# Routing and NSA stages of a hybrid decoder layer: zeros written by ScalarE, the second gate's modulation moved, products issued in pairs, other issue orders

## The chip, the cores and the metric

One core of a Trainium2 chip runs the whole layer as one program. The metric is device microseconds (us) of one execution. The engines are TensorE (PE in the profile, with its weight loads as PEld), VectorE (DVE), ScalarE (ACT), GpSimd (POOL), SyncE (SP, which only issues DMAs here). Each engine runs its own queue in the order in which the program put the instructions; an instruction that waits holds up all that stand behind it on its engine.

## The reference

512 tokens of width 1024 pass through one layer in fp32. Cut to its outline:

```python
mod = silu(c) @ ada_w + ada_b
sh1, sc1, gt1, sh2, sc2, gt2 = split(mod, 6)
h = ln(x) * (1 + sc1) + sh1
z = h @ w_in                          # columns of three mixers
o_a = mla_attention(...)              # 4 heads
o_b = banded_window_attention(...)    # 4 heads, window 128, sinks
o_c = nsa_attention(...)              # 8 heads, 2 KV groups: g0*compressed + g1*selected + g2*window
x = layernorm(ALPHA * x + (1 + gt1) * (concat[o_a, o_b, o_c] @ w_out))
h = ln(x) * (1 + sc2) + sh2
x = layernorm(ALPHA * x + (1 + gt2) * moe(h))   # 16 experts in 4 groups, one group, two experts of it
```

The selected branch of NSA takes for each query the 8 best of 16 key blocks; here it is computed densely, over all causal keys with a mask. The router's choice decides which expert sees which token.

## The kernel before

The tokens stand in four blocks of 128 (n = 0 to 3). The stages follow each other: modulation and layer norm, projections with MLA and window attention, the NSA stage (function `nsa(n)`, queries of a block by `queries(n)`), the output projection with the second layer norm and the routing of each block (`outproj(n)`, which calls `route(n)`), and the experts (a loop over four expert groups q). A scheduler turns the program into one queue for each engine: it goes by program order, shifted by priorities (`pri`, whose numbers stand in `PRM`), by what is ready in its own model of time, and by free buffers. `tc.issue_after(ins)` puts what follows behind `ins` on the same engine. The order of the stages' pieces is the string `ORD`: q is a query block, n an NSA block, o an output block, s steps of the first modulation iterator, g steps of `gstep`; what stands behind Z comes after the buffers of the projections are freed.

In `nsa(n)` the 8 heads fall into two groups g. For each block: window scores (L849) and softmax; `nl`, the choice of blocks and the masks `msk` (L882); `np`, the window part of the output, with products of V and the transposed probabilities (function `pv`, L894); then for g = 0 and 1 in turn the selected part: scores (L921), softmax into the tile `Sg` (L490, L491, scaled in L133), for each key block kt four transposes (`stp`, L501), their copy from PSUM into a tile `pt` (L127), and `pv`. All products of a block add up in one PSUM bank (`onsa`), group 0 in partitions 0 to 63 and group 1 in 64 to 127: each `pv` uses 64 of the array's 128 columns. The products with `vz` are the compressed branch.

The second gate (gt2, needed at the end of the experts) is `m3`: two steps of `mod_half`, each with two groups of four matmuls (`gemv`, L323, `modps`) on four loaded tiles of ada_w (`ada`, L192) and two additions on VectorE (L548). The tiles come from the pool `zraw` (tag w, 5 buffers), which also holds the raw halves of W_out (`wo`, L966) for its split into `woh` and `wol`, the gate tile gt1, and later gt2 and four tiles `x1g`. The two steps are called by `step(16, gsteps)` behind the last output block. `s2 s1 s2 s2` in the last part of `ORD` call an iterator that has six steps, all of which have been taken by then.

`outproj(n)` multiplies the heads' outputs by W_out (`yps`, L1215: `oM` part in fp32, `oN` part split in `oh` and `ol`), normalizes on VectorE (L1217 to L1233), transposes (`x1p`), copies to `x1T` on ScalarE, computes the router's logits (`lps`, `lsum`) and writes the normalized rows to DRAM (`t2`, L1238 and L1240). `route(n)` is a chain of some fifty small VectorE instructions with three products on TensorE between them: `rkp` (ranks, L1097), `tabp` (L1129) and `tabq` (L1163, L1165). After block 3, `tokB` (L1131) lists the tokens of the experts' second and third slots. `warm` adds products whose result nobody reads.

The experts' loop gathers rows (`gather`, an indirect DMA of POOL, L1289) into the tiles `rows`, transposes them (`gTp`), and computes gate and up (`gu`, L1319: for each of 8 k, for each of 3 slots b, four matmuls side by side), then down (`dn`). Slot b = 0 holds tokens of the first two blocks and is known after block 1 (`tokA`); b = 1 and 2 need `tokB`. The rows of a gather that no token fills must be zero: POOL clears `rows` 1 and 2 (L1272) and the first two pairs of `x1g` (L1327, L1328).

## Time and profile before

| | us |
|---|---|
| median of 3 runs | 593.4 |
| the runs | 591.91, 593.4, 599.62 |
| the profiled execution | 596.7 |
| its span, first to last instruction | 594.8 |
| busy in the span: PE, DVE, ACT, POOL | 548.7, 368.2, 222.1, 97.4 |
| NSA stage and output projection with routing of the first blocks | 234 to 384.6 |
| last block's norm and routing, up to its first expert product of slot 1 | 384.6 to 423.3 |
| experts | 423.3 to 584 |

The execution that was profiled took 596.7 us; 1.9 us of it lie around the span. A busy PE counts the modelled ends of pipelined matmuls, so neighbouring matmuls overlap in the sums of single durations; the busy time of a stretch counts each moment once. A matmul in fp32 stands as two records.

### The profile page before, as it was taken

Reading aid. Unit: us, or ns where it says so; the run is one execution under the profiler, and the core shown is the slowest. Engines: PE = TensorE matmul, PEld = TensorE weight load, DVE = VectorE, ACT = ScalarE, POOL = GpSimd, SP = SyncE. Lnnn points to the kernel's source line nnn. Section 1 sums busy time; section 2 is a strip of 40 time slices with the busy share of each in tenths; the row PEclk is TensorE's granted clock in tenths of the full one; section 3 lists DMA queues with packets and bytes.
Section 4 is the critical chain, followed back from the end, with each engine's and each line's share of the span. In section 5 each row is a group of like instructions: output and inputs, shape, how many; then the busy total and the mean of one; then the engine's idle time right before and its main releaser. Section 6 shows DMA issues by size and latency. Waiting matters only on the chain.

```text
span 594.8 us, 10444 instructions
## 1 busy us (share of the span) xinstructions
PE 548.7 (92%) x3856; PEld 333.1 (56%) x3856; DVE 368.2 (62%) x1219; ACT 222.1 (37%) x556; POOL 97.4 (16%) x114
## 2 busy tenths in 40 slices
PE   2899999999899999999899999978899999999990
PEld 1559775687788998755455456653434234234240
DVE  7515656664678568877769568886138157167174
ACT  2514443561428336374634512121434062070130
POOL 0114200000010010003301112123502122011022
PEclk9969999999799999999999999978999999999996
DMA  8993246743930200098300685359699999999601
GB/s 301 373 328 108 83 142 225 260 153 102 323 91 19 72 37 1 2 220 226 124 2 0 222 278 200 119 209 306 164 370 351 366 365 348 374 356 354 248 1 47
DMA packets 77546, 117.05 MB, mean 197 GB/s; under 512 B 7937, under 2 KB 54440, under 8 KB 77492
## 3 DMA queue, kind: packets, MB, share of 16 engines
q1 hardware_dynamic: 72328, 102.60, 52.9%
q0 software_dynamic: 4960, 13.64, 6.3%
q8 instruction: 32, 0.52, 0.4%
q14 instruction: 22, 0.18, 0.1%
q10 hardware_dynamic: 204, 0.11, 0.1%
HBM read 112.12 MB, written 8.40 MB: 203 GB/s over the span
## 4 chain that ended last, share of the span: by engine, by line
PE 78%; DVE 11%; issue 3%; DMA 3%; ACT 2%; POOL 2%; ACTq 0%; POOLq 0%
PE gu L1319 13%; PE zps L407 13%; PE dn L1370 7%; PE onsa L894 6%; PE yps L1215 5%; PE zall L423 3%; PE modps L323 2%; PE modps L375 2%; PE gTp L997 2%; PE cmb L1410 2%; PE stp L501 2%; PE sps L921 2%; PE wps L849 1%; PE warm L356 1%; PE cmh L1418 1%
## 5 line engine op out<-in xcount | busy, mean ns | idle before, releaser
L1319 PE MATMUL gu<-gu,gT 128*32 128x512 f32 x768 | 85.3, 596 | 0.1
L1319 PEld LDWEIGHTS gu<-gu,gT 128*32 128x32 f32 x768 | 23.8, 110 | 52.5 <-issue 50.6
L1370 PE MATMUL dn<-dn,aT 128*32 128x512 f32 x384 | 45.3, 597 | 0.4 <-ACT aT L127 0.2
L1343 DVE TENSOR_TENSOR act<-act,gu 128x256 f32<-128x256 f32 x12 | 5.1, 421 | 59.8 <-ACT act L1342 59.8
L1002 ACT ACTIVATE gT<-gTp,modc,modc 128x128 f32<-128x128 f32 x96 | 35.7, 461 | 10.1 <-PE gTp L997 9.5
L1342 ACT ACTIVATE act<-gu 128x256 f32<-128x256 f32 x12 | 4.6, 387 | 72.1 <-PE gu L1319 72.1
L1215 PE MATMUL yps<-wol,oM 128*128 128x512 f32 x64 | 30.9, 595 | 0.0
L1375 DVE SCALAR_TENSOR_TENSOR y<-dn,tab,gt 128x512 f32<-128x512 f32 x24 | 18.0, 748 | 10.2 <-PE dn L1370 10.2
L323 PE MATMUL modps<-ada,cond 128*32 128x512 f32 x128 | 18.3, 631 | 4.4 <-DVE gr L1079 4.1
L1370 PEld LDWEIGHTS dn<-dn,aT 128*32 128x32 f32 x384 | 10.4, 109 | 20.8 <-issue 18.5
L894 PE MATMUL onsa<-pt,vs 128*64 128x512 f32 x40 | 20.6, 614 | 0.0
L491 ACT ACTIVATE Sg<-Sg,nms 128x128 f32<-128x128 f32 (+3 forms) x32 | 17.8, 559 | 3.7 <-DVE nms L490 3.3
L491 ACT ACTIVATE W<-W,nmw 128x256 f32<-128x256 f32 (+1 forms) x32 | 15.3, 478 | 9.7 <-DVE nmw L490 9.3
L997 PEld LDWEIGHTS gTp<-cf,rows 128*128 128x128 f32 x96 | 10.4, 142 | 15.1 <-ACT gT L1002 9.2
L448 DVE TENSOR_TENSOR rp<-zps,trig 128x128 f32<-128x128 f32 (+1 forms) x28 | 9.7, 345 | 12.9 <-PE zps L407 12.5
L356 PE MATMUL warm<-cf 128*128 128x128 f32 x88 | 17.2, 326 | 0.1
L407 PE MATMUL zps<-B1s,hH 128*128 128x256 f32 x64 | 15.1, 329 | 2.2 <-DVE B1s L210 1.1
L356 PEld LDWEIGHTS warm<-cf 128*128 128x128 f32 x88 | 13.8, 222 | 5.5 <-issue 4.7
L1378 DVE TENSOR_TENSOR ys<-y,ys 128x512 fp32r<-128x512 f32 x22 | 15.2, 692 | 2.1 <-ACT ys L127 1.4
L997 PE MATMUL gTp<-cf,rows 128*128 128x128 f32 x96 | 14.8, 282 | 1.6 <-DMA rows<-xs_d,tokB 1.6
L127 ACT COPY pt<-stp 128x512 f32<-128x512 f32 x14 | 7.9, 586 | 22.2 <-PE stp L501 21.9
L1389 ACT ACTIVATE R<-R,rsf 128x1024 f32<-128x1024 f32 x3 | 3.7, 1241 | 31.4 <-DVE rsf L1388 31.4
(529 smaller groups left out, 1472.7 us busy)
## 6 DMA issues: line engine op xcount, KB each, us to landing
ada<-in_ada_w_dram SPq DMA_DIRECT2D x48, 512.0 KB, 5.9
gu<-in_moe_w_gate_dram SPq DMA_DIRECT2D x32, 512.0 KB, 9.7
gu<-in_moe_w_up_dram SPq DMA_DIRECT2D x32, 512.0 KB, 9.6
dn<-in_moe_w_down_dram SPq DMA_DIRECT2D x16, 1024.0 KB, 10.5
x<-in_x_dram SPq DMA_DIRECT2D x4, 512.0 KB, 4.9
phik<-in_nsa_phi_k_dram SPq DMA_DIRECT2D x4, 512.0 KB, 5.0
phiv<-in_nsa_phi_v_dram SPq DMA_DIRECT2D x4, 512.0 KB, 4.8
wo<-in_w_out_dram SPq DMA_DIRECT2D x8, 256.0 KB, 9.3
```

The source lines that it names most:

```text
L323: return lambda: PE.matmul(ps[32 * j:32 * j + 32], cond[:, k], t[:, 512 * (j % 2):512 * (j % 2) + 512], start=first, stop=last, skip_group ...
L356: PE.matmul(ps[:, :128], ident, ident, start=True, stop=True)
L407: PE.matmul(ps[:, :w], l[:, k, ts_], get(k, r), start=(k == 0 and i == 0), stop=(k == KD - 1 and i == 2))
L423: m = PE.matmul(outs[n], l[:, k, n * 128:(n + 1) * 128], get(k, r), start=(beg and n % 2 == 0), stop=(k == KD - 1 and i == 2), skip_group_ ...
L491: S.activation(S_h, S_h, AF.Exp, bias=nm, scale=-1.0, accum_out=den)
L894: PE.matmul(ops[64 * g:64 * g + 64, cols], lhsT, rhs, start=first[g], stop=False, skip_group_check=True)
L997: PE.transpose(ps[:, k * 128:(k + 1) * 128], src[:, (4 * a + k) * 128:(4 * a + k + 1) * 128], ident)
L1002: S.activation(dst[:, kk], pk, AF.Identity, bias=sh2(kk), scale=sc2(kk))
L1215: last = PE.matmul(ps, l, r[:, cs], start=(i == 0), stop=(i == len(order) - 1))
L1319: together([lambda e=e: PE.matmul(gu[b][32 * e:32 * e + 32], gT[b][:, k, 32 * e:32 * e + 32], w[:, e], start=(k == 0), stop=(k == KD - 1), ...
L1370: together([lambda b=b, e=e, f=f: PE.matmul(dn[b][32 * e:32 * e + 32], aT[b][:, f, 32 * e:32 * e + 32], wd[f][:, e], start=(f == 0), stop= ...
L1375: V.scalar_tensor_tensor(y, dn[b], tab[:, s:s + 1], gt2[:, cs], op0=OP.mult, op1=OP.mult)
```

## The change

ScalarE writes the zeros (as a product of a constant tile with 0.0) that POOL wrote. The second gate's two steps are taken as `g1` before and after the NSA block 2 in `ORD`; the first call of `gstep` flushes the first iterator and makes `m3`. The empty steps go. In `nsa(n)` the selected part computes the scores and the softmax of both groups first and then, for each key block, transposes both and issues the two products one behind the other (`pv2`); the window and compressed products are tied in pairs too. The `pt` tiles in the NSA stage become four, the mask tiles two. `t2` on ScalarE is issued behind the copies to `x1T`. The gate and up products of q = 0 with k >= 3 are issued behind the last `tabq` product.

```diff
-    "ORD": "q0 q1 n0 n1 q2 q3 s1 n2 Z n3 o0 s2 s1 s2 o1 o2 s2 o3 L", "SWb": 2, "WF": 2, "aTe": "S", "c10": -600,
+    "ORD": "q0 q1 n0 n1 q2 q3 s1 g1 n2 g1 Z n3 o0 o1 o2 o3 L", "SWb": 2, "WF": 2, "aTe": "S", "c10": -600,
...
-    "gst1": 80, "gst2": 40, ... "mskb": 3, ... "ptbs": 2, "ptbw": 2,
+    "gst1": -40, ... "mskb": 2, ... "ptbs": 4, "ptbw": 4,
...
                 def pv(g, lhsT, rhs, cols):
-                    PE.matmul(ops[64 * g:64 * g + 64, cols], lhsT, rhs, start=first[g], stop=False, skip_group_check=True)
+                    m = PE.matmul(ops[64 * g:64 * g + 64, cols], lhsT, rhs, start=first[g], stop=False, skip_group_check=True)
                     first[g] = False
+                    return m
+
+                def pv2(v, pts, cols):
+
+                    m = pv(1, v[:, 64:128], pts[1], cols)
+                    with tc.issue_after(m.ins), tc.high_priority():
+                        pv(0, v[:, 0:64], pts[0], cols)
...
                     pts = [tposed(qp, SW[g][:, :, b * 128:(b + 1) * 128], "wtp") for g in range(2)]
-                    for g in range(2):
-                        pv(g, vw[:, w0 + b, 64 * g:64 * g + 64], pts[g], slice(0, 512))
+                    pv2(vw[:, w0 + b], pts, slice(0, 512))
...
                 for r in range(4):
-                    for g in range(2):
-                        pv(g, vz[:, 4 * g + r], cpt, qs(r))
-
+                    m = pv(0, vz[:, r], cpt, qs(r))
+                    with tc.issue_after(m.ins), tc.high_priority():
+                        pv(1, vz[:, 4 + r], cpt, qs(r))
+
+            Sgs = []
             for g in range(2):
...
-                    for kt in range(n + 1):
-                        pt = tposed(qp, Sg[:, :, kt * 128:(kt + 1) * 128], "stp")
-                        pv(g, vs[:, kt, 64 * g:64 * g + 64], pt, slice(0, 512))
+            with pri(f"nv{n}"):
+                for kt in range(n + 1):
+                    pts = [tposed(qp, Sgs[g][:, :, kt * 128:(kt + 1) * 128], "stp") for g in range(2)]
+                    pv2(vs[:, kt], pts, slice(0, 512))
...
+        gsteps = []
+
+        def gstep(n):
+
+            if not gsteps:
+                step(16)
+                gsteps.extend((mod_bias(10, 2), 0))
+                gsteps[1] = mod_half(gsteps[0], 1)
+            step(n, gsteps[1])
...
-        m3 = mod_bias(10, 2)
-        gsteps = mod_half(m3, 1)
...
-            warm(f"wT{n}", PE.matmul(tq[:, 2 * NSLOT:2 * NSLOT + 8], ohg, rg, start=False, stop=True, skip_group_check=True))
+            tabq.append(PE.matmul(tq[:, 2 * NSLOT:2 * NSLOT + 8], ohg, rg, start=False, stop=True, skip_group_check=True))
+            warm(f"wT{n}", tabq[-1])
...
-                    cp(pick("x1T", "SS", hf), x1T[:, 4 * hf:4 * hf + 4], heads(ps, 4))
+                    x1c = S.copy(x1T[:, 4 * hf:4 * hf + 4], heads(ps, 4))
...
-            S.activation(t2, x1, AF.Identity, bias=nm, scale=rs2)
+            with tc.issue_after(x1c.ins):
+                S.activation(t2, x1, AF.Identity, bias=nm, scale=rs2)
...
+        def zero(dst):
+
+            S.mul(dst, cf[:, :dst.shape[-1]], 0.0)
+
         for r in rows_[1:]:
-            G.memset(r, 0.0)
+            zero(r)
         cnt_w = [0]
-        step(16, gsteps)
-        gate_out(1, m3)
+        gstep(16)
+        gate_out(1, gsteps[0])
...
-                for b in range(CAPB):
-                    together([lambda e=e: PE.matmul(gu[b][32 * e:32 * e + 32], gT[b][:, k, 32 * e:32 * e + 32], w[:, e],
-                                                    start=(k == 0), stop=(k == KD - 1), skip_group_check=True)
-                              for e in range(4)])
+
+                with tc.issue_after(tabq[-1].ins) if q == 0 and k >= 3 else nullcontext():
+                    for b in range(CAPB):
+                        together([lambda e=e: PE.matmul(
+                            gu[b][32 * e:32 * e + 32], gT[b][:, k, 32 * e:32 * e + 32], w[:, e],
+                            start=(k == 0), stop=(k == KD - 1), skip_group_check=True) for e in range(4)])
...
                 if q < 2:
-                    G.memset(x1g, 0.0)
-                    G.memset(x2g, 0.0)
+                    zero(x1g)
+                    zero(x2g)
```

## Rows read from the trace of the kernel before

**Rows 1.** The page: busy time of PE and DVE in the span, and the chain that ended last by engine.
```profile
PE 548.7 (92%) x3856; PEld 333.1 (56%) x3856; DVE 368.2 (62%) x1219; ACT 222.1 (37%) x556; POOL 97.4 (16%) x114
...
PE 78%; DVE 11%; issue 3%; DMA 3%; ACT 2%; POOL 2%; ACTq 0%; POOLq 0%
```

**Rows 2.** Busy time by stretch: bounds, length, then busy us (instructions) of PE, PEld, DVE, ACT, POOL, the granted clock of TensorE, DMA share and GB/s.
```profile
234.00:384.60 150.60, 147.01 (x762) 88.42 (x760) 113.80 (x470) 64.56 (x166) 29.04 (x28) 1.00 0.45 133
384.60:402.50 17.90, 13.83 (x107) 8.68 (x107) 15.02 (x71) 5.41 (x12) 4.17 (x6) 0.81 0.58 214
402.50:408.70 6.20, 3.53 (x32) 1.46 (x24) 5.93 (x19) 1.29 (x2) 4.18 (x6) 1.00 0.99 326
408.70:416.20 7.50, 7.44 (x46) 3.58 (x46) 3.58 (x32) 0.00 (x0) 0.00 (x0) 0.77 1.06 331
416.20:423.30 7.10, 5.39 (x49) 4.23 (x45) 2.33 (x11) 0.90 (x3) 3.62 (x6) 1.00 0.54 126
```

**Rows 3.** Groups of TensorE instructions by line in the stretch 243 to 347: busy us, mean ns of one, idle before.
```profile
L894 PE MATMUL onsa<-pt,vs 128*64 128x512 f32 x40 | 20.6, 614 | 0.0
...
L501 PE MATMUL stp<-cf,Sg 128*128 128x128 f32 x80 | 12.7, 283 | 1.6 <-DVE Sg L133 1.6
...
L894 PE MATMUL onsa<-pt,vw 128*64 128x512 f32 x28 | 11.3, 618 | 0.0
...
L894 PE MATMUL onsa<-cpt,vz 128*64 128x128 f32 x64 | 6.3, 284 | 0.0
...
L1215 PE MATMUL yps<-woh,oh 128*128 128x512 f32 x14 | 6.2, 440 | 0.0
```

**Rows 4.** Timeline of TensorE: products of both groups side by side, one product alone, all eight products of a compressed branch, eight transposes.
```profile
282.33 1.08 PE L894 MATMUL onsa<-pt,vw 128*64 128x512 f32 x4
...
294.24 1.07 PE L894 MATMUL onsa<-pt,vs 128*64 128x512 f32 x2
...
286.73 1.09 PE L894 MATMUL onsa<-cpt,vz 128*64 128x128 f32 x16
...
299.07 1.09 PE L501 MATMUL stp<-cf,Sg 128*128 128x128 f32 x8
```

**Rows 5.** Timeline of ScalarE: a copy of transposed probabilities from PSUM.
```profile
341.60 0.59 ACT L127 COPY pt<-stp 128x512 f32<-128x512 f32 x1 [1.80 <-PE stp L501]
```

**Rows 6.** Timeline of TensorE: the first two entries of the second gate's products, and the last block's logits.
```profile
384.63 1.92 PE L323 MATMUL modps<-ada,cond 128*32 128x512 f32 x16
...
390.63 1.94 PE L323 MATMUL modps<-ada,cond 128*32 128x512 f32 x8 [4.07 <-DVE gr L1079]
...
399.58 0.64 PE L1244 MATMUL lps<-x1T,rwc 128*32 128x128 f32 x16
```

**Rows 7.** VectorE instructions on the tile `mod` in the stretch 384.6 to 402.5 (columns as in rows 2, without ACT and POOL).
```profile
384.60:402.50 17.90, 0.00 (x0) 0.00 (x0) 3.14 (x5) 0.81 0.58 214
```

**Rows 8.** Timeline of ScalarE around the last block's copies.
```profile
394.02 1.24 ACT L1238 ACTIVATE t<-yt,ynm,yrs 128x1024 f32<-128x1024 f32 x1 [10.19 <-DVE key L1099]
...
395.17 1.05 ACT L127 COPY x1T<-x1p 128x512 f32<-128x512 f32 x2
```

**Rows 9.** Timeline of VectorE: `aff` in block 2's routing and in block 3's, the last inputs of block 3's products, and its token list.
```profile
384.17 0.17 DVE L1142 TENSOR_SCALAR aff<-th 128x16 f32<-128x16 f32 x1
...
402.63 4.08 DVE L1142 TENSOR_SCALAR aff<-th 128x16 f32<-128x16 f32 x1
...
411.80 0.23 DVE L1157 TENSOR_SCALAR r<-oht,gr 128x24 f32<-128x24 f32 x1
...
416.87 0.17 DVE L1131 TENSOR_TENSOR tokB<-tab,tabp 128x12 int32<-128x12 f32 x1 [4.45 <-PE tabp L1129]
```

**Rows 10.** Timeline of POOL: the first two and the last of the six memsets.
```profile
402.10 1.86 POOL L1272 MEMSET rows<- 128x1024 f32 x2
...
406.14 0.54 POOL L1328 MEMSET x1g<- 128x512 f32 x1
```

**Rows 11.** Timeline of TensorE from block 3's `rkp` products to its `tabp`, without some entries between.
```profile
405.65 0.38 PE L1096 MATMUL rkp<-asg,ones 128*128 128x20 f32 x2
...
408.76 0.40 PE L1097 MATMUL rkp<-asg,cf 128*128 128x20 f32 x2 [2.73 <-DVE asg L1088]
...
410.18 2.50 PE L356 MATMUL warm<-cf 128*128 128x128 f32 x10
...
414.36 1.92 PE L1319 MATMUL gu<-gu,gT 128*32 128x512 f32 x16
...
416.21 0.61 PE L1129 MATMUL tabp<-rh,ohp 128*128 128x12 f32 x4
```

**Rows 12.** The chain of waits at the gather, and all gathers into `rows`: from issue to landing.
```profile
417.79 4.25 DMA rows<-xs_d,tokB
...
DMA to landing us min/median/max: 4.2/6.2/7.1
```

**Rows 13.** Timeline of SP's queue: the later seven loads of W_out's raw halves, and the second gate's tiles.
```profile
257.82 6.33 SPq L966 DMA_DIRECT2D wo<-in_w_out_dram  x7
...
278.13 14.59 SPq L192 DMA_DIRECT2D ada<-in_ada_w_dram  x4
...
385.33 2.19 SPq L192 DMA_DIRECT2D ada<-in_ada_w_dram  x4
```

More of the change, by code (lines that the diff above doesn't have):

```diff
@@ L910, in nsa @@
                 for r in range(4):
-                    for g in range(2):
-                        pv(g, vz[:, 4 * g + r], cpt, qs(r))
+                    m = pv(0, vz[:, r], cpt, qs(r))
+                    with tc.issue_after(m.ins), tc.high_priority():
+                        pv(1, vz[:, 4 + r], cpt, qs(r))
+            Sgs = []
             for g in range(2):
                 with pri(f"ns{n}"):
-                    Sg = qp.tile([128, 4, 512], F32, name="Sg", bufs=pr("Sgb", 2))
+                    Sg = qp.tile([128, 4, 512], F32, name="Sg", bufs=2)
+                    Sgs.append(Sg)
                     nm, dn = tiny("nms"), tiny("dns")
@@ L938, in run @@
                     f[t[0]][0](int(t[1]))
-        outproj = gstep = None
+        gsteps = []
[5 more added lines that the diff above has]
+            step(n, gsteps[1])
+        outproj = None
         ORD = pr("ORD", "q0 n0 q1 n1 s1 q2 q3 Z n2 n3 L o0 o1 o2 g1 o3 g1")
@@ L1057, in build @@
         base = rp.tile([128, 20], F32, name="base")
+        tabq = []
         def route(n, lps, rs):
```

4 lines of the change are left out of this document (1 added, 3 removed), and 6 rows, old and new, of the table PRM.

## The prediction, made before the changed kernel was run

> **What bounds the kernel now.** I read the page first: TensorE is busy for 92% of the span and holds 78% of the chain that ended last [rows 1]. Such a mean hides stages with other limits, so the next view is the busy time by stretch. From 234 to 384.6 us (NSA, output projection, routing of the first blocks) TensorE is busy for 147.0 of 150.6 us, VectorE for 113.8 [rows 2]. The reader is to see that there an engine's work counts, not a chain's latency: a microsecond of TensorE saved is a microsecond at most, while VectorE leaves room. In the 38.7 us from 384.6 to 423.3 it is the other way round. That is block 3's norm and routing, and nothing but its end (the token list, the gather, the transposes) lets the experts go on. There the waits count: VectorE is busy for 15.0 of 17.9 us and then for 5.9 of 6.2, then it idles while TensorE is busy, then both wait for a DMA [rows 2]. The experts behind 423.3 are left as they are, so what is won before moves them forward as a whole.
>
> **The products in pairs.** One product of 64 columns takes 1.07 us alone, and two of different groups take 1.08 us together [rows 4]. The selected part's 20 products are all issued alone or behind one of the same group: 20.6 us busy (40 records). As ten pairs they take 10 x 1.08 = 10.8, so 9.8 less. The 14 window products take 11.3 us; seven pairs are 7.6, so 3.7 less. The compressed products take 6.3 us; four branches at the best one's 1.09 are 4.4, so 1.9 less [rows 3, 4]. Together 15.4; some of these intervals overlap (the three groups add up to 38.2 us, and the moments counted once are a little fewer), so I take 14.7.
>
> **The gate's modulation, moved.** In the NSA stretch TensorE gets four groups of four matmuls more; two take 1.92 us [rows 6], so 3.8. VectorE gets 3.1 us there [rows 7]. Eight loads of 512 KB go with it on SP's queue; four were issued in that stretch already, at 278, and held four of the five `zraw` buffers until 384.6, four at 385.3 [rows 13]. The DMA share of the stretch is 0.45 [rows 2], so transfer time is covered; what it costs if the buffers run out is the rival below. Net for TensorE: 14.7 - 3.8 = 10.9 us.
>
> How much of that is time? Now both softmaxes of a block must be finished before the first selected product, so the first group's products no longer cover the second group's softmax. Transposes wait 1.6 us for the scaled `Sg` once in the old order [rows 3]; I charge about 1 us for each of four blocks, 4 us. VectorE would hold 113.8 + 3.1 = 116.9 us in some 140, still below TensorE. So the stretch gives **7 us**. Bounds: nothing, if the new waits eat all, and 10.9, the whole of the work.
>
> **Block 3's norm.** The moved work leaves the stretch 384.6 to 402.5: 3.1 us on VectorE, which is busy there for 15.0 of 17.9, and on TensorE products behind a wait of 4.07 us, with the norm's transposes queued behind them [rows 2, 6]. The wait is put to a VectorE instruction; I read it as the four tiles issued at 385.3 [rows 13]. The first group after it took 1.94 us where two groups had taken 1.92; the granted clock is 0.81 in this stretch [rows 2, 6]. Here ScalarE also wrote `t2` (1.24 us) before the copies to `x1T`, and the logits came at 399.58 [rows 6, 8]; now the copies go first, and the write of `xs_d` starts some 1 us later, 20 us before it is read. Bounds: nothing, if the interleaved routing of block 2 sets the pace, and 6, the two waits behind `modps` with the 1.24. VectorE's is the nearest row: **3.5 us**.
>
> **The zeros.** `aff` took 0.17 us in block 2 and 4.08 in block 3, from 402.63 to 406.71, and POOL's six memsets run from 402.10 to 406.68 [rows 9, 10]. VectorE stood still for them, 3.9 us. With ScalarE writing they go. ScalarE has 1.29 us of work in 402.5 to 408.7 and none in the 7.5 us after it [rows 2]; six products of at most 1.24 us (the 1024 wide activation [rows 8]) are under 7.5 us and are covered, unless one is issued before the routing's own tanh, which then waits 1.2. TensorE has products queued before `rkp` until 406.0 [rows 11], so `rkp` moves from 408.76 to 406.0 at best: **3 us**, bounds 0 (if it meets the next wait at once) and 3.9. The Trainium skill ("SBUF — State Buffer", section SBUF: two separate sides) says that VectorE and GpSimd take the shared port pair as an exclusive lock for one whole instruction. By that alone the wait would be one memset, some 1 us, and the sum 2 us smaller, which lies inside the main case. The rows show VectorE passed over for all six.
>
> **The products held back.** `tabp`'s inputs are there at 412.0, and it starts at 416.21: 12 `warm` records and `gu` products of slot 0 with k = 3 to 6 stand before it [rows 9, 11]. With k >= 3 behind `tabq`, only the warm ones (2.5 us for ten) stand between `rkp` and `tabp`: **4.1 us**. The five `gu` groups held back (16 records 1.92, so about 5 us) then fall into the wait for the gather; if TensorE's clock is at its half level then, they take up to 10.
>
> **What they collide with.** The gather took 4.25 us, in a stretch with a DMA share of 0.54; in the 14 us before it the share is 0.99 to 1.06, with weights, gate and norm rows on SP's queue [rows 2, 12]. That traffic starts when block 3's buffers go free, so it does not move against the routing, but the gather comes some 7 us earlier relative to it and meets its last part. Gathers into `rows` have a median of 6.2 and a maximum of 7.1 us [rows 12]: I give back **2 us**, bounds 0 and 2.9.
>
> The other edits (empty steps, mask and `pt` buffers) move no work; four `pt` tiles let a pair wait for its two copies without holding up the next transposes.
>
> **Sum.** 7 + 3.5 + 3 + 4.1 - 2 = 15.6 us. Against the profiled execution's 596.7 us that is 581.1. That execution lies 3.3 us above the median of 593.4, and the runs spread from 591.9 to 599.6, so against the median it is **578 us**.
>
> **Rivals.**
> *Only the routing gains.* NSA's new waits eat the pairs: For it: the selected transposes do wait for `Sg`; against it: TensorE has output products to fill with, some 18 us of the split kind alone before 347 (three kinds of 14 records, 6.2 us for one [rows 3]). Then 8.6 us are left: 585.
> The Trainium skill ("TensorEngine Tiling (Array Packing)", section PSUM Bottleneck) says that side by side products speed up TensorE but not the copies out of PSUM, which may become the bound. As a mechanism here: a pair needs two copies of 0.59 us, 1.2 us on ScalarE alone, while its transposes and products take 2 x 1.09 + 1.08 = 3.3 us on TensorE [rows 4, 5], so the copies have more than twice the room. Should they bind all the same, the pairs bring nothing and it ends at 585 too.
> *The routing gives its gain back.* The gather meets full DMA traffic, `gu` at half clock runs past its landing, or weights k = 6 and 7 come late; TensorE's clock of 0.77 in 408.7 to 416.2 speaks for it [rows 2]. Held-back products at 10 us against some 8 of gather cost 2, the gather's maximum 0.9 more, and a zero before the tanh 1.2: 4.1 less, 582.
> *Slower.* The gate's eight tiles come before W_out's raw halves in program order and share five buffers. If SP's queue waits for the gate's products before it may load `wo`, issued at 258 now [rows 13], the split part of the output products has no weights; the 18 us of them fill TensorE before 347 now. If all of them are pushed behind NSA, TensorE idles instead, the pairs count for nothing, and 18 - 8.6 = 9.4 us are lost: 603. It decides from 8.6 us of such idling on.
>
> **How the numbers follow.** Main case 0.62, with a range of its own from 570 (all of 10.9, routing 11) to 586; only the routing gains 0.20; copies out of PSUM 0.03; routing gives back 0.09; slower 0.06. From 568 to 590 the range holds all but the slow case and the edges of the others. Faster by over 2% means below 581.5 (2% is about what a measurement of this kernel can tell from no change): four fifths of the main case (0.50) and a quarter of the three that end at 582 to 585 (0.08 of 0.32): 0.58. Slower by over 2% means above 605.3: 0.03. The rest, 0.39, is within 2%.
>
> **What would show it.** After: the selected products stand as four records of some 1.08 us; the NSA stretch is some 7 us shorter with TensorE still nearly full; no `modps` behind the last `yps`; `aff` of block 3 takes 0.17 us; from `rkp` to `tabp` it is 3 to 4 us and not 7.5; the gather takes about 6 us. The sum is wrong if TensorE shows idle time behind `Sg` or `woh` in the NSA stretch, if `gu` of slot 0 is still running when the gather has landed, or if the experts' loop no longer takes the same time from one group to the next.

## The result, and the profile after

| | before | after |
|---|---|---|
| median of the runs | 593.06 us (4 runs, 591.91 to 599.62) | 588.45 us (4 runs, 584.61 to 593.21) |
| ratio, 95% interval | | 0.9898 [0.9852, 0.9945] |
| profiled execution, its span | 596.7, 594.8 us | 588.79, 587.0 us |

The change is faster by 1.0%, 4.6 us, where 15.6 were forecast. In this document medians are of all runs, while ratios, their intervals and mean clocks leave out runs more than 1.5% above the fastest of their kernel, and no stretches are given where the profiled execution is such a run. The page after, busy time and chain by engine:

```profile
PE 534.9 (91%) x3856; PEld 327.8 (56%) x3856; DVE 364.9 (62%) x1219; ACT 227.4 (39%) x562; POOL 92.7 (16%) x108
...
PE 71%; DVE 14%; DMA 7%; issue 4%; ACT 2%; POOL 2%; ACTq 0%; POOLq 0%; DVEq 0%
```

TensorE lost 13.8 us of busy time against [rows 1], and the span only 7.8: TensorE's part of the chain fell from 78 to 71%. Busy time by stretch (columns as in [rows 2]): NSA stage, block 3's norm, its routing, the gather, the first expert group:

```profile
234.00:384.20 150.20, 139.53 (x778) 84.64 (x776) 115.62 (x472) 66.58 (x164) 27.86 (x27) 1.00 0.48 151
384.20:399.40 15.20, 10.60 (x73) 7.92 (x73) 11.30 (x62) 7.83 (x14) 3.70 (x5) 0.78 1.03 346
399.40:405.90 6.50, 5.12 (x42) 3.87 (x40) 5.53 (x49) 0.22 (x1) 0.00 (x0) 1.00 0.26 101
405.90:412.90 7.00, 6.07 (x53) 3.08 (x53) 2.06 (x11) 0.34 (x1) 4.62 (x7) 1.00 0.39 95
412.90:451.30 38.40, 38.40 (x309) 16.27 (x308) 15.40 (x30) 17.48 (x47) 8.01 (x9) 1.00 0.96 326
```

The first row is the finding: 7.5 us less TensorE work than in [rows 2], 10.7 us of idle time where there were 3.6, and the same length. Both windows start at 234, though, and the second execution is 1.9 us ahead there. Cut at the same work (from the compressed keys' last product to W_out's last product), before and then after, the stretch has 5.7 us less work, 7.1 us more idle time, and is 1.4 us longer, at the full granted clock both times:

```profile
250.70:384.20 133.50, 129.96 (x633) 73.46 (x632) 98.46 (x401) 57.05 (x139) 27.57 (x26) 1.00 0.50 149
...
248.80:383.70 134.90, 124.24 (x663) 71.88 (x663) 102.27 (x408) 60.18 (x142) 27.12 (x26) 1.00 0.53 167
```

The 7.8 us of the whole span are found by laying the same milestones on both timelines (us; start of the last instruction of the kind):

| from one milestone to the next | before | after | difference | predicted |
|---|---|---|---|---|
| start to the compressed keys' last product | 250.7 | 248.8 | -1.9 | 0 |
| to W_out's last product (NSA stage) | 133.5 | 134.9 | +1.4 | -7 |
| to the last logits' sums, `lsum` (block 3's norm) | 17.5 | 15.7 | -1.8 | -3.5 |
| to the table, `tabp` | 14.9 | 6.9 | -8.0 | -7.1 (zeros 3, held 4.1) |
| to the first `gu` after that block's gather | 6.7 | 6.6 | -0.1 | +2 |
| to the next expert group's first `gu` | 35.9 | 38.4 | +2.5 | 0 |
| to the end | 135.7 | 135.7 | 0 | 0 |

The table's first row is not what the change is about: both programs issue the same TensorE instructions there, in the same order but for the first block's window products at its end, and the clock was granted otherwise (0.77 and 1.00 in the stretch 150 to 165). The routing's rows on TensorE, after, are to be read against [rows 6, 11]:

```profile
398.09 0.62 PE L1261 MATMUL lps<-x1T,rwc 128*32 128x128 f32 x16
...
399.42 0.29 PE L1268 MATMUL lsum<-cf,x1T 128*128 128x16 f32 x2
...
405.92 0.61 PE L1144 MATMUL tabp<-rh,ohp 128*128 128x12 f32 x4 [1.26 <-DVE rh L1141]
...
411.86 1.09 PE L1011 MATMUL gTp<-cf,rows 128*128 128x128 f32 x8 [0.91 <-DMA rows<-xs_d,tokB]
412.88 1.92 PE L1342 MATMUL gu<-gu,gT 128*32 128x512 f32 x16
```

The gather itself took 4.32 us (4.25 before [rows 12]). A pair takes the 1.08 us that it was priced at [rows 4], but not all came out as pairs: in the first block's window part and at one of block 1's keys the two products stand apart, each 1.07 us alone. Timeline of TensorE, after, then the three groups of products (columns as in [rows 3]) and one of the gate's four groups in the stage:

```profile
299.58 1.08 PE L894 MATMUL onsa<-pt,vs 128*64 128x512 f32 x4
...
L894 PE MATMUL onsa<-pt,vs 128*64 128x512 f32 x40 | 11.9, 618 | 1.0 <-ACT pt L127 0.7 <-DVE pt L127 0.3
L894 PE MATMUL onsa<-pt,vw 128*64 128x512 f32 x28 | 8.6, 618 | 0.0
L894 PE MATMUL onsa<-cpt,vz 128*64 128x128 f32 x64 | 4.7, 279 | 0.0
...
277.54 1.06 PE L323 MATMUL modps<-ada,cond 128*32 128x512 f32 x8
```

The waits of TensorE for `Sg` grew from 1.6 us [rows 3] to 4.1; these waits in 234 to 350, after (us in total, times, longest):

```profile
PE stp L501 <- DVE Sg L133: 4.1, 4, 1.8
```

Two of the four, 1.85 and 1.82 us, are both in block 2, and most of the other idle time up to 350 is short waits for VectorE's part of the softmaxes (`nms`, `nmw`, `W`) and for `pt`. The chain of waits in the NSA stage, after (start, us, what), shows what they wait on:

```profile
260.87 0.64 DVE mod L548
...
262.53 0.69 DVE mod L548
...
265.58 0.33 DVE W L490
...
270.58 0.33 DVE W L490
...
272.78 2.10 DVE W L133 x8
...
291.53 1.93 DVE dns L934
...
295.10 2.86 DVE Sg L133 x2
```

From 260.87 to 275.69 and from 287.41 to 298.01 the chain runs mostly through VectorE; the moved gate's own additions (`mod`) stand on it too. Followed back over the whole stage (its 195 longest pieces), it has 102 us on TensorE and 26 on VectorE before, 64 and 41 after. Two things may feed this; the experiments test them. W_out's raw halves are loaded 21 us later than in [rows 13], so that the first output product, a filling for such waits, stands at 287.88 and not at 261.95. SyncE's queue, after:

```profile
278.65 10.49 SPq L986 DMA_DIRECT2D wo<-in_w_out_dram  x8
```

And GpSimd's splits of these halves (`wol`, L999) run beside the softmax of block 2 (before, the one at 290.0 did so, with the 1.6 us wait behind it), where an operation of 128x4, 0.17 us a little later, takes 2.01. Timeline of GpSimd and VectorE, after:

```profile
291.08 2.35 POOL L999 TENSOR_TENSOR wol<-wo,woh 128x1024 fp32r<-128x1024 f32 x1 [0.92 <-ACT woh L127]
...
291.45 2.01 DVE L934 TENSOR_TENSOR dns<-dns,gat 128x4 f32<-128x4 f32 x1
```

### The profile page after: what moved, and what is told of

Same layout as the page of the kernel before. It is cut to its first block, busy times and chain, and to the rows that moved or that the text cites. A ratio compares the mean times of both kernels' runs of the same rounds, so it can differ in the third digit from the quotient of the medians.

```text
span 587.0 us, 10441 instructions
## 1 busy us (share of the span) xinstructions
PE 534.9 (91%) x3856; PEld 327.8 (56%) x3856; DVE 364.9 (62%) x1219; ACT 227.4 (39%) x562; POOL 92.7 (16%) x108
## 4 chain that ended last, share of the span: by engine, by line
PE 71%; DVE 14%; DMA 7%; issue 4%; ACT 2%; POOL 2%; ACTq 0%; POOLq 0%; DVEq 0%
PE gu L1342 14%; PE zps L407 12%; PE dn L1393 8%; PE onsa L894 3%; PE yps L1231 3%; PE zall L423 3%; PE modps L323 3%; DMA ada<-in_ada_w_dram 2%; PE gTp L1011 2%; PE cmb L1433 2%; PE modps L375 2%; PE wps L849 1%; PE warm L356 1%; PE stp L501 1%; PE cmh L1441 1%
## 5 line engine op out<-in xcount | busy, mean ns | idle before, releaser
L501 PE MATMUL stp<-cf,Sg 128*128 128x128 f32 x80 | 13.8, 286 | 4.1 <-DVE Sg L133 4.1
L501 PEld LDWEIGHTS stp<-cf,Sg 128*128 128x128 f32 x80 | 8.9, 140 | 14.5 <-issue 9.3
L1231 PEld LDWEIGHTS yps<-wol,oM 128*128 128x128 f32 x64 | 11.5, 191 | 8.1 <-issue 7.7
L356 PE MATMUL warm<-cf 128*128 128x128 f32 x88 | 15.7, 307 | 0.1
## 6 DMA issues: line engine op xcount, KB each, us to landing
gu<-in_moe_w_up_dram SPq DMA_DIRECT2D x32, 512.0 KB, 10.1
```

The lines of the kernel that those rows point to most:

```text
L356: PE.matmul(ps[:, :128], ident, ident, start=True, stop=True)
L501: PE.transpose(ps[:, h * 128:(h + 1) * 128], Ssl[:, h], ident)
L1231: last = PE.matmul(ps, l, r[:, cs], start=(i == 0), stop=(i == len(order) - 1))
```

## The experiments

Each table gives the median, the ratio to the kernel before measured beside it, with its interval (before's medians were 594.7 to 595.4), the lengths of three stretches in the profiled execution, and the mean granted clock of the runs. The stretches: NSA as above; "routing", from W_out's last product to `tabp`; "rest", from `tabp` to the last `gu`. Before: 133.5, 32.4, 146.0, clock 0.970; changed kernel: 134.9, 22.6, 148.5, clock 0.973.

**The halves of the change.** `gate_at_end` is the changed kernel with the gate where it was; `no_pairs` the changed kernel with the old products; `pairs_alone` and `routing_alone` put one half onto the kernel before.

`gate_at_end`, against the changed kernel (and the gate's functions as before):

```diff
-    "ORD": "q0 q1 n0 n1 q2 q3 s1 g1 n2 g1 Z n3 o0 o1 o2 o3 L"
+    "ORD": "q0 q1 n0 n1 q2 q3 s1 n2 Z n3 o0 o1 o2 o3 L"
```

`no_pairs`, against the changed kernel, and `pairs_alone` with the same lines the other way, against the kernel before (buffers with them):

```diff
-                    pv2(vw[:, w0 + b], pts, slice(0, 512))
+                    for g in range(2):
+                        pv(g, vw[:, w0 + b, 64 * g:64 * g + 64], pts[g], slice(0, 512))
...
```

`routing_alone`, against the kernel before:

```diff
-            G.memset(r, 0.0)
+            zero(r)
...
+                with tc.issue_after(tabq[-1].ins) if q == 0 and k >= 3 else nullcontext():
...
+            with tc.issue_after(x1c.ins):
```

> The changed kernel with the second gate's modulation back behind the last output block. Theory A (displaced loads): the pairs do shorten the NSA stretch, but the gate's tiles hold the zraw buffers, W_out's raw halves come 26 us later, their splits on GpSimd fall on block 2's softmax, and this eats the pairs' 7 us. Then the NSA stretch gets 7 us back and block 3's norm loses about 3.5: some 585 us. Theory B (chain, not work): the NSA stretch ends with a chain of softmaxes over VectorE and ScalarE and a tail of fixed length, so that TensorE work taken out turns into idle time. Then only the 3.5 us are lost: some 592 us.

> The changed kernel with the products of P and V as before (no pairs, two pt tiles, three mask tiles, each group's softmax followed by its own products). Theory A: the pairs' 7 us are missing, and the late loads stay: some 595 us. Theory B: TensorE was not what ended the stretch, so no change, 587 to 590 us.

> The kernel before with the pairs alone (with their buffers). Theory A: 7 us less than before, some 586 us, with W_out's loads at 252 as before. Theory B: no change, 592 to 594 us, TensorE some 10 us more idle between 234 and 384.

> The kernel before with the three routing edits alone: zeros from ScalarE, gate and up products with k >= 3 behind tabq, t2 behind the copies to x1T; the gate's modulation stays at its old place. Both theories: 3 + 4.1 us for the first two, up to 1 for the third, less up to 2 for the gather: 586 to 588 us. If it reaches 589 or more, the gate's move is worth more in block 3's norm than 1 us.

| | median | ratio | NSA | routing | rest | clock |
|---|---|---|---|---|---|---|
| gate_at_end | 596.24 | 1.0007 [0.997, 1.0043] | 129.9 | 28.5 | 153.2 | 0.956 |
| no_pairs | 603.1 | 1.0126 [1.004, 1.0211] | 144.8 | 25.5 | 149.3 | 0.955 |
| pairs_alone | 600.56 | 1.0107 [1.0039, 1.0174] | 133.5 | 35.7 | 151.2 | 0.954 |
| routing_alone | 595.36 | 1.0001 [0.9966, 1.0035] | 133.4 | 25.9 | 156.1 | 0.969 |

Neither half gains anything by itself, and both first theories (A, the displaced loads; B, a chain, not work) missed, but for B's 592 us in `gate_at_end`, which as a ratio to its 593 lies within the interval. The rows say why. In `routing_alone` the routing is 6.5 us shorter, and the experts' stretch 10.1 longer: the tokens come earlier, but the gather takes 9.24 us, and the clock falls behind the wait for it (0.50 from 414 to 420). SyncE's queue had stood at the store of the gate's row, with the weights of k = 6 and 7 (four loads of 512 KB) behind it. Timeline of `routing_alone`, SyncE's queue and TensorE:

```profile
394.73 0.51 SPq L345 DMA_DIRECT2D gt_d<-mod  x1
...
395.30 0.39 SPq L1323 DMA_DIRECT2D gu<-in_moe_w_gate_dram  x1
...
414.57 1.97 PE L997 MATMUL gTp<-cf,rows 128*128 128x128 f32 x8 [5.83 <-DMA rows<-xs_d,tokB]
```

In `pairs_alone` GpSimd's memsets hold up the inputs of block 2's table: TensorE waits 3.99 us, and goes on at half clock, which its mean 0.59 in 399 to 404 shows. (Ahead of this it waits 5.1 us for a tile of the gate.) Timeline of TensorE in `pairs_alone`:

```profile
399.03 0.61 PE L1139 MATMUL tabp<-rh,ohp 128*128 128x12 f32 x4 [3.99 <-DVE rg L1170]
```

Busy time of `pairs_alone` by stretch (columns as in [rows 2]):

```profile
394.00:399.00 5.00, 1.04 (x12) 0.13 (x4) 5.00 (x4) 1.51 (x5) 4.94 (x7) 1.00 0.39 124
399.00:404.00 5.00, 4.97 (x30) 4.27 (x30) 1.38 (x5) 0.00 (x0) 0.00 (x0) 0.59 0.22 51
```

And with the pairs but without the gate's tiles, the NSA stage loses clock in two places. In `gate_at_end` two splits in a row on GpSimd stretch eight VectorE operations to 6.39 us (2.10 in the changed kernel), a copy behind them is late, TensorE waits 2.93 us, and its next products run at half clock; at 328.77 it waits 3.02 us more for a softmax. Timeline of VectorE, GpSimd and then TensorE in `gate_at_end`:

```profile
270.13 6.39 DVE L133 TENSOR_SCALAR W<-W,rw 128x256 f32<-128x256 f32 x8
...
271.19 4.91 POOL L995 TENSOR_TENSOR wol<-wo,woh 128x1024 fp32r<-128x1024 f32 x2 [2.19 <-ACT woh L127]
...
277.24 1.11 PE L501 MATMUL wtp<-cf,W 128*128 128x128 f32 x4 [2.93 <-DVE pt L127]
278.28 1.98 PE L894 MATMUL onsa<-pt,vs 128*64 128x512 f32 x4
...
328.77 1.97 PE L501 MATMUL stp<-cf,Sg 128*128 128x128 f32 x8 [3.02 <-DVE Sg L133]
```

**The late weights, the pairs with the gate, W_out's loads.** From here on the theories are C (pairs and gate need each other: the pairs make room in the NSA stage, the gate's leaving brings the weights out of the gather's way) and D (only the clock differs).

The two `..._gate_queue`, against `routing_alone` and `gate_at_end` (the load of the row likewise):

```diff
-            SP.dma_start(gt_d[2 * i:2 * i + 2], r[0:64:32])
+            (G if i == 1 else SP).dma_start(gt_d[2 * i:2 * i + 2], r[0:64:32])
```

`gate_after_wout`, against the changed kernel; `pairs_and_gate` and `gate_moved_alone` put the change's own lines for these parts, and the new order, onto the kernel before:

```diff
-    "ORD": "q0 q1 n0 n1 q2 q3 s1 g1 n2 g1 Z n3 o0 o1 o2 o3 L"
+    "ORD": "q0 q1 n0 n1 q2 q3 s1 n2 Z g1 n3 g1 o0 o1 o2 o3 L"
```

> The kernel before with the four routing edits (empty steps gone, zeros from ScalarE, products held back, t2 behind the x1T copy), as in routing_alone, and one edit more: the store and the load of the gate's row (gt_d) are issued on GpSimd's DMA queue and not on SyncE's. In routing_alone SyncE's queue waited with that store until 394.73, and the weights of k = 6 and 7 stood behind it (395.30 to 398.2); their 4 MB and the norm rows were still moving when the second block's gather started, and it took from 404.4 to 414.6 where the changed kernel's took 4.3. Theory C (late weights meet the gather): with the store out of the queue the weights go at about 382, the gather takes 4.3 to 5 us, the first transposes come about 5 us earlier, and the clock does not fall to half in 414 to 420: 5 to 8 us, a ratio to before of 0.987 to 0.992. Theory D (what differs between these kernels is only where the clock falls): gather shorter or not, ratio 0.997 to 1.003.

> The changed kernel without the gate's move (gate_at_end), and the store and load of the gate's row on GpSimd's DMA queue. gate_at_end's gather ended in a wait of 3.2 us at 414.77, with the clock at half from 400 to 410. Theory C: tokens at 404.8 and a gather of 4.3 us bring the first transposes to about 410.5, 4 us earlier; ratio to before 0.990 to 0.995, about the changed kernel's without moving the gate at all. Theory D: the clock falls in 400 to 410 all the same and the ratio stays at 0.997 to 1.004.

> The kernel before with the pairs and the gate's move (and the empty steps gone), without the other routing edits: zeros from GpSimd, products not held back, t2 free. Theory C: the NSA stage ends as in the changed kernel; routing loses the zeros' stall (3.9) and the held-back products again, while the gather no longer meets late weights; 4 to 6 us over the changed kernel, ratio 0.997 to 1.001. Theory D, by which the routing edits are worth nothing (as routing_alone's 1.0001 reads by itself): 0.988 to 0.992.

> The changed kernel with the gate's eight tiles after W_out's raw halves and not before them (the order of the NSA stage is s1 n2 Z g1 n3 g1 o0 and not s1 g1 n2 g1 Z n3 o0). In the changed kernel W_out's loads went out at 278.65 (before 252 to 264), GpSimd's splits of them ran from 287.8 to 302, and two VectorE operations of n2's softmax took 2.01 and 3.18 us beside them while TensorE waited 1.85 and 1.82. Theory A (the displaced loads): the splits come back to about 270 to 285, these two waits and the idle time of 260 to 280 go, 3 to 5 us; ratio to before 0.981 to 0.985. Rival (the waits move to other softmaxes, the stage's end is set by the chain of VectorE): as the changed kernel, 0.987 to 0.992.

> The kernel before with the gate's move alone (and the empty steps gone): no pairs, no other routing edit. Theory C: the NSA stage, whose TensorE has no free time, gets about 11 us longer as in no_pairs (from the end of the compressed keys' products to W_out's last product 145 against 133.5), block 3's norm and the gather lose 5 to 6: ratio to before 1.006 to 1.012. Rival (the gate's work hides, the pairs give all of the gain in pairs_and_gate): 0.99 to 1.0.

| | median | ratio | NSA | routing | rest | clock |
|---|---|---|---|---|---|---|
| routing_alone_gate_queue | 588.86 | 0.9913 [0.9877, 0.9949] | 133.5 | 25.8 | 148.9 | 0.975 |
| gate_at_end_gate_queue | 594.0 | 1.0008 [0.9969, 1.0048] | 133.2 | 29.0 | 149.6 | 0.955 |
| pairs_and_gate | 587.8 | 0.9895 [0.986, 0.993] | 133.6 | 26.6 | 146.1 | 0.969 |
| gate_after_wout | 590.89 | 0.9925 [0.9889, 0.9961] | | | | 0.971 |
| gate_moved_alone | 599.95 | 1.0085 [1.0047, 1.0123] | 143.6 | 25.8 | 146.0 | 0.962 |

One store on another queue turns `routing_alone` from nothing into 0.9%: the gather takes 4.79 us and its wait 1.39, as theory C had it. From the chain of waits of `routing_alone_gate_queue`:

```profile
410.36 4.79 DMA rows<-xs_d,tokB
```

With pairs in the kernel the same edit brings nothing (`gate_at_end_gate_queue`): the gather's wait is gone, but TensorE stood 2.67 us for `asg` at 401, and the clock is at half from 404 to 412. There theory C failed, and D's range was met. It was so in `pairs_and_gate` too: C had put it at 0.997 to 1.001, and D, by which the routing edits are worth nothing, at 0.988 to 0.992. C was met by `routing_alone_gate_queue` and `gate_moved_alone`. And 0.9895 is the changed kernel's 0.9898: beside the pairs and the gate's move the other routing edits bring nothing that these intervals could show. The square of pairs and gate is clear: gate alone +0.85%, pairs alone +1.07%, both -1.05%. The gate's tiles cost 10.1 us in a stage that has no free TensorE time (143.6 against 133.5), and next to nothing beside the pairs (133.6 against the 133.5 of `pairs_alone`). The granted clock of the stage is 0.95 in `pairs_alone` and 1.00 in `pairs_and_gate`, so that, as I read it, beside the pairs the tiles stand where time was lost to the clock. The stage in both:

```profile
245.20:378.60 133.40, 122.15 (x632) 73.30 (x631) 99.83 (x396) 57.38 (x138) 27.46 (x26) 0.95 0.50 149
...
252.30:385.90 133.60, 123.84 (x664) 72.38 (x663) 101.68 (x407) 57.96 (x139) 29.90 (x29) 1.00 0.55 170
```

`gate_after_wout` was to show what the late output products cost, and could not: the first one came later still, at 304.45, behind the gate's products in the program's order; its ratio lies near its rival's range.

**The splits and the held products.**

`..._splits_on_vector`, against the kernel named (`gate_at_end` here is the one with its gate's row on GpSimd's queue):

```diff
-    "woE": "GG"
+    "woE": "VV"
```

`..._nothing_held`, against the kernel named:

```diff
-                with tc.issue_after(tabq[-1].ins) if q == 0 and k >= 3 else nullcontext():
-                    for b in range(CAPB):
+                for b in range(CAPB):
```

> gate_at_end_gate_queue with W_out's four splits of the low parts on VectorE and not on GpSimd. In gate_at_end two of them stood back to back on GpSimd (271.19, 4.91 us); beside them eight VectorE operations of 128x256 took 6.39 us where one takes 0.34 elsewhere (2.7 for eight), a copy behind them came late, TensorE waited 2.93 us at 277.24, and the clock was at half from 277.5 to 280. Theory E (the splits hold VectorE, the wait lets the clock fall, and so the room that the pairs make is lost): without GpSimd's splits 3.7 us of VectorE time and about 1.5 of half clock come back against four splits of about 1.1 us on VectorE: 1 to 3 us, ratio to before 0.995 to 0.999. Rival (VectorE has no room: its busy share in these stretches is 0.9 to 1): 1.000 to 1.005.

> The changed kernel with W_out's four splits on VectorE and not on GpSimd. In the changed kernel they ran at 287.8 to 302.8; a 128x4 operation of n2's softmax took 2.01 us and three of 128x384 took 3.18 beside them, and TensorE waited 1.85 and 1.82 us. Theory E: these two waits go and four splits of about 1.1 us come onto VectorE: 0 to 3 us less, ratio to before 0.985 to 0.990. Rival (VectorE has no room there): 0.990 to 0.995.

> The kernel before with W_out's four splits on VectorE, nothing else. Theory E with the chain of waits (in the kernel before 100 of the NSA stage's 134 us ran through TensorE and 30 through VectorE, so that GpSimd's hold on VectorE is mostly hidden; with the pairs VectorE has 43 to 48): within 1.5 us of before, ratio 0.998 to 1.002. Rival (the splits on GpSimd cost the same in both kernels, and the pairs have no part in it): 0.993 to 0.997.

> The changed kernel without the products held back: the first group's products with k >= 3 don't wait for the table of the last block. My prediction priced the held products at 4.1 us. Theory F (what is held is only moved): the table comes later by 2 to 4 us, but TensorE has the products done while it waits for the gather, and the first expert group takes 36 us and not 38.4: within 1.5 us of the changed kernel, ratio to before 0.987 to 0.992. Rival (the prediction's 4.1 stands): 0.995 to 0.998.

> changed_splits_on_vector without the products held back. Theory F (what is held is only moved): as changed_splits_on_vector, 0.983 to 0.988. Rival (the held products are worth their 4.1 us once the waits of the stage are gone): 0.990 to 0.993.

| | median | ratio | NSA | routing | rest | clock |
|---|---|---|---|---|---|---|
| gate_at_end_splits_on_vector | 590.94 | 0.9944 [0.9906, 0.9982] | 128.9 | 31.1 | 148.5 | 0.956 |
| changed_splits_on_vector | 586.88 | 0.985 [0.9797, 0.9903] | | | | 0.974 |
| before_splits_on_vector | 600.95 | 1.0105 [1.0075, 1.0134] | 131.1 | 37.8 | 148.9 | 0.960 |
| changed_nothing_held | 596.08 | 0.9897 [0.9819, 0.9974] | | | | 0.972 |
| changed_splits_on_vector_nothing_held | 589.26 | 0.9903 [0.9866, 0.9939] | 132.5 | 24.9 | 146.1 | 0.964 |

Theory E (the splits hold VectorE) is borne out where the pairs are: with the splits off GpSimd the ratios are 0.5 to 0.6% lower, though in both pairs of kernels the intervals overlap; the stage takes 128.9 us in `gate_at_end` where two profiles with the splits on GpSimd have 129.9 and 133.2. Theory F (what is held is only moved) is met by `changed_nothing_held`, but by two runs only (586.79 and 590.15; the other four took 596 to 597 us), and missed by the other one, which lies in its rival's range. In the kernel before, taking the splits off GpSimd makes the stage 2.4 us shorter as well (131.1, against 133.4 to 133.5 in three kernels with the old stage), so that their cost is not the pairs' doing alone, as I had expected; but the kernel loses 1%, which neither theory had. Its routing meets the memsets as `pairs_alone` did: VectorE is held for 4.97 us there, and TensorE waits 3.99, and 5.7 for a tile of the gate before that. Timeline of VectorE and GpSimd in `before_splits_on_vector`:

```profile
399.61 4.97 DVE L1160 TENSOR_SCALAR rg<-cf,v 128x8 f32<-128x8 f32 x1
...
399.94 0.97 POOL L1327 MEMSET x1g<- 128x1024 f32 x1
400.83 1.86 POOL L1272 MEMSET rows<- 128x1024 f32 x2
402.61 0.54 POOL L1328 MEMSET x1g<- 128x512 f32 x1
403.08 0.97 POOL L1327 MEMSET x1g<- 128x1024 f32 x1
403.98 0.54 POOL L1328 MEMSET x1g<- 128x512 f32 x1
```

The Trainium skill ("SBUF — State Buffer", section SBUF: two separate sides) has VectorE and GpSimd take their shared ports as an exclusive lock for one instruction. The traces agree that VectorE stands still, but here it was passed over for six memsets in a row (4.97 us) and for two splits (6.39 us), not for one instruction.

**Putting it together.** `gate_between_blocks` keeps W_out's loads ahead and has the gate's tiles inside the stage; the next one adds the splits on VectorE and holds nothing; the last two each put one routing edit back to its other state.

```diff
-    "ORD": "q0 q1 n0 n1 q2 q3 s1 g1 n2 g1 Z n3 o0 o1 o2 o3 L"
+    "ORD": "q0 q1 n0 n1 q2 q3 s1 n2 Z n3 o0 g1 o1 g1 o2 o3 L"
```

And `..._zeros_on_gpsimd`, against the second:

```diff
-            zero(r)
+            G.memset(r, 0.0)
...
```

> The changed kernel with the gate's eight tiles behind the output products of blocks 0 and 1 (the order is s1 n2 Z n3 o0 g1 o1 g1 o2 o3 and not s1 g1 n2 g1 Z n3 o0 o1 o2 o3): W_out's loads go out ahead of them and its products come before theirs in the accumulators' banks. In the changed kernel the first output product was at 287.88 and the chain of waits ran through VectorE from 260.87 to 275.7 and from 287.4 to 298, with no product to fill; in gate_after_wout the output products came even later (304.45), behind the gate's accumulators. Theory G (what the stage lost are the output products as a filling): they start at about 255 to 262, the NSA stage takes 131 to 132 us and not 134.9, routing stays; 2 to 4 us under the changed kernel, ratio to before 0.983 to 0.987. Rival (VectorE sets the stage, whatever fills TensorE): 0.988 to 0.993.

> gate_between_blocks with W_out's four splits on VectorE and without the products held back. Theory G with E: another 1 to 3 us, ratio to before 0.977 to 0.984, the fastest of all. Rival: as changed_splits_on_vector, 0.985 or above.

> gate_between_blocks_splits_on_vector with the products held back again (so it is the changed kernel, the gate between the blocks, the splits on VectorE, and nothing else). Theory F (what is held is only moved): the stretch before the second block's gather not shorter by more than 1 us, the first expert group 38.4 us and not 36; ratio to before 0.980 to 0.986, that is 0 to 3 us over gate_between_blocks_splits_on_vector's 0.9807. Rival (the held products are worth the prediction's 4.1 us, as changed_splits_on_vector_nothing_held's 0.9903 against 0.985 may be read): 0.972 to 0.976.

> gate_between_blocks_splits_on_vector with the zeros of the gathered rows and of the experts' buffers from GpSimd's memsets again, as before the change; nothing held back. Theory H (once the gate is out of the routing stretch the memsets run beside W_out's last products or block 3's norm and the stall of VectorE hides; the gate's move has taken what the prediction gave to the zeros): 0.979 to 0.984. Rival (the zeros are worth the prediction's 3 us in their own right): 0.985 to 0.989.

| | median | ratio | NSA | routing | rest | clock |
|---|---|---|---|---|---|---|
| gate_between_blocks | 589.11 | 0.992 [0.9893, 0.9947] | 133.4 | 23.8 | 149.5 | 0.963 |
| gate_between_blocks_splits_on_vector | 584.7 | 0.9807 [0.9769, 0.9846] | 130.9 | 25.4 | 147.7 | 0.967 |
| between_blocks_splits_and_held | 586.17 | 0.9861 [0.9812, 0.991] | 129.7 | 23.8 | 149.5 | 0.963 |
| between_blocks_splits_zeros_on_gpsimd | 591.83 | 0.9952 [0.9906, 0.9998] | 133.2 | 27.5 | 146.2 | 0.960 |

Theory G fell: early output products alone (`gate_between_blocks`) do not shorten the time. The wait for a copy behind two of GpSimd's splits is there again, 2.94 us. Timeline of TensorE in `gate_between_blocks`:

```profile
276.66 0.66 PE L501 MATMUL wtp<-cf,W 128*128 128x128 f32 x4 [2.94 <-DVE pt L127]
```

With these on VectorE and nothing held, the kernel takes 584.7 us (I call it the best kernel below), 1.9% under before, and its interval lies just below the changed kernel's. Its longest waits of TensorE in 234 to 350 (us in total, times, longest):

```profile
PE stp L501 <- DVE Sg L133: 1.6, 2, 0.8
PE onsa L894 <- ACT pt L127: 0.9, 2, 0.7
PE wps L849 <- DVE nmw L490: 0.9, 2, 0.6
```

Holding products again (`between_blocks_splits_and_held`) makes the routing 1.6 us shorter and the rest 1.8 longer, as theory F has it; 0.9861 is at the edge of its range. Putting the zeros back onto GpSimd costs 1.45% (0.9952 against 0.9807), more than the 3 us of the prediction and than either theory's range, and theory H fell with it. The three stretches of the table account for 2.9 us of these 8.6; the profiled executions do not show where the rest is lost. The table of block 2 waits for VectorE again. Timeline of TensorE in `between_blocks_splits_zeros_on_gpsimd`:

```profile
398.00 0.62 PE L1143 MATMUL tabp<-rh,ohp 128*128 128x12 f32 x4 [1.87 <-DVE r L1171]
```

## Why the prediction was right or wrong

**The NSA stage: this step failed.** "So the stretch gives 7 us" was 10.9 us less work, minus 4 us of new waits. Measured between the same milestones it was 5.7 us less work and 7.1 more idle time, that is 1.4 lost: both terms were mis-sized, and it is the same sum that turned over.

The work: the three groups of products gave 13.0 us (38.2 in [rows 3], 25.2 after) where 14.7 were taken, and the gate's four groups cost 4.2 (1.06 each, issued singly) and not 3.8. That makes 8.8, a little of it ahead of the stage; why the busy time of the stage fell by 5.7 only is open.

The waits: I charged 1 us for `Sg` in each block, since "VectorE would hold 116.9 us in some 140, still below TensorE". A mean busy share hides the chain inside a block. 3.7 of the 4.1 us for `Sg` are two waits in block 2, each beside one of GpSimd's splits, and most of the other new waits are for other steps of the softmaxes and for copies: VectorE's part of the stage's chain grew from 26 to 41 us. What the runs show of the cause is the splits: without them on GpSimd the stage is 1.0 to 4.3 us shorter in `gate_at_end_splits_on_vector` and 2.4 in the kernel before, and with the output products early as well, in the best kernel, VectorE's part of the chain is 25 us, as before the change. There the stage is 2.6 us shorter than before, with 124.2 us of work and 6.7 idle, 3.2 more than before. So the waits need not cost more than the 4 us charged; what is missing there is the work, 5.8 us less and not 10.9, some of it because the clock is at half for a while (0.97 over the stage). Busy time in the best kernel, the stage and then 6 us of it at half clock:

```profile
247.80:378.70 130.90, 124.17 (x665) 72.44 (x664) 101.89 (x411) 59.58 (x142) 18.80 (x22) 0.97 0.58 174
...
330.00:336.00 6.00, 5.73 (x17) 2.19 (x17) 0.00 (x0) 1.39 (x3) 0.00 (x0) 0.50 0.00 0
```

The clock is no part of the changed kernel's loss: its stage has 1.00, as before. It is what the pairs lose without the gate's tiles in the stage: the mean of the whole runs is 0.954 to 0.956 in all four such kernels, against 0.970 before. Time multiplied by mean clock, averaged over the runs, is an estimate of the time at full clock: 576.5 us before, 569.2 in `gate_at_end`. So by this estimate the pairs and the routing edits took some 7 us of full-speed time away there, and the lower clock gave it back.

Two of the prediction's own signs of being wrong came: TensorE idle behind `Sg`, and an expert group that takes longer. Of the signs of being right, `aff` of block 3 takes 0.17 us, `rkp` to `tabp` 3.1, and no `modps` stands behind the last `yps`.

**The gate.** Its price on TensorE, 3.8 us, was too low where TensorE has no room (10.1 us in `gate_moved_alone`, the displaced output products among them); beside the pairs it is hidden by what the clock gives back. The displaced loads of W_out were my slower rival, 9.4 us lost. The loads came 21 us late, but not at that price: `gate_between_blocks` takes them back and is not faster than the changed kernel.

**Block 3's norm** gave 1.8 and not 3.5 us: TensorE's wait of 4.07 us behind the gate's products [rows 6] is gone, but one of 4.55 us for the norm's `yt` stands in its place, and the clock is as low behind it (0.78 over the stretch, 0.81 before [rows 2]). Timeline of TensorE, after:

```profile
388.82 1.97 PE L1247 MATMUL x1p<-cf,yt 128*128 128x128 f32 x8 [4.55 <-DVE yt L1244]
```

**Zeros and held products**: `lsum` to `tabp` became 8.0 us shorter against 7.1, but that is luck as to these two edits. `pairs_and_gate` and `gate_moved_alone` have neither, and the same step is 7.4 us in both, in the changed kernel 6.9: the gate's leaving does it. I added what overlaps: from W_out's last product to `tabp` it is 32.4 us before, 25.8 with the gate's move alone, 25.9 with the routing edits alone, and 22.6 with all; and against `pairs_and_gate` the 4.0 us that the routing edits win there are lost again in the experts (2.4) and the stage (1.3). The held products are only moved: what is held runs in the first expert group, 38.4 us with them (412.88 to 451.32) and 35.8 in `pairs_and_gate` (419.34 to 455.17). That is the +2.5 of the table, for which the sum had no term, since I let them vanish in the wait for the gather. In the best kernel holding them costs 0.5% (the intervals overlap); in `changed_splits_on_vector` the medians say the contrary, within overlapping intervals, so a small effect of either sign stays open. The zeros on GpSimd cost most where TensorE waits behind the memsets (8.6 us by ratio, 2.9 by the stretches, in the best kernel; 3.99 us of TensorE's wait in `pairs_alone`); in `pairs_and_gate` they hold VectorE for 2.77 us and TensorE does not wait for it.

**The collision** was no 2 us but nothing: the gather took 4.32 us. The mechanism is real, 9.24 us of gather in `routing_alone`; but I wrote that this traffic "does not move against the routing", and it does: without the gate's store in front of them the weights go out at 384.16, and the DMA share is 0.26 and 0.39 around the gather, not 0.99 to 1.06 ahead of it as in [rows 2].

**Against the median.** The profiled execution before lay 3.3 us over its median, the one after 0.3, and 1.9 us of its gain come from the clock ahead of the change. Of the rivals "only the routing gains" (585) was nearest, and in what it says of the stage right: new waits ate the pairs. 585 plus the 2.5 of the expert group is 587.5, measured 588.45; that the zeros and held products are not what gained makes part of the agreement luck.

## What to carry to other kernels

Side by side products take work from TensorE, but here the stage was no shorter by it: read the chain of waits inside the stage, not its busy shares, see what TensorE waits for during each softmax, and what else holds VectorE then. Edits against one wait do not add: put each alone onto the old kernel and take each alone out of the new one. A step moved off a queue also moves what stood behind it, which was worth 0.9% in `routing_alone`.

## What the runs showed of the hardware beyond what was expected

A wait of TensorE of about 3 us is often followed by the half level of its clock: behind 2.93 us at 277.24 and 3.02 at 328.77 in `gate_at_end` (0.62 in 276 to 280, 0.52 and 0.63 in 328 to 336), behind 3.99 us at 399.03 in `pairs_alone` (0.59 in 399 to 404). The full-speed time lost in these stretches, their length by what is missing of the clock, is 1.5, 3.4 and 2.1 us: a wait of three or four us costs half as much to a little more than as much again. The fall came without so long a wait too: in the best kernel two of 0.8 us close together, which ended at 327.32 and 328.73, were followed by 0.50 in 330 to 336. The mean clock goes with the time within one kernel too: of 19 runs of the kernel before, a span of 589.6 us has 0.977 and one of 597.3 has 0.963. The part ahead of the change, nearly the same in all kernels, ended between 244.8 and 252.9 us in the profiled executions, so single profiles are to be compared from a common milestone on.
